# Trace of a batched matrix product: A resident per batch, two adjacent rows per partition, B streamed by row tile

## The chip, the cores and the metric

The kernel runs on one core of one Trainium2 chip. The metric is device time in microseconds (us), the median of several executions. A profile shows a span that is about 1.7 us shorter than the timed execution, because it runs from the first to the last instruction.

Some words: TensorE is the engine for matrix products and, here, for transposes; it writes into a memory called PSUM, from which VectorE reads. GpSimd issues the transfers. A row tile is 128 rows of a matrix, one per partition of the on-chip memory. A descriptor is the order to move one contiguous run of bytes. A landing is the record that a part of a transfer has arrived. The granted clock is TensorE's, as a share of full speed.

## The reference

```python
def setup_inputs():
    B, N = 8, 2176
    # a, b: random normal, float32, shape (8, 2176, 2176)

def reference(a, b):
    prod = np.matmul(a, b)
    traces = np.diagonal(prod, axis1=1, axis2=2).sum(axis=-1)
    return traces.astype(np.float32)
```

The trace of A·B is the sum over all i and j of A[i, j]·B[j, i]. No matrix product is needed. One of the two matrices must be transposed, multiplied with the other element by element, and summed. All of A and B must be read: 303.04 MB in fp32.

## The kernel before

N is 17 tiles of 128 (NT = 17). A whole row tile is one transfer, which casts fp32 to bf16 on the way. B comes in groups of four row tiles, with buffers for two groups. TensorE transposes 128x128 blocks of B into PSUM, and VectorE multiplies four of them with 512 columns of A and sums.

```python
    KGW = 4                                  # row tiles of B in a group
    a_pool = ctx.enter_context(tc.tile_pool(name="a_pool", bufs=2 * NT))
    b_pool = ctx.enter_context(tc.tile_pool(name="b_pool", bufs=2 * KGW))
    psum_pool = ctx.enter_context(tc.tile_pool(name="psum", bufs=7, space=bass.MemoryType.PSUM))
    # ... (cut)
    for bi in range(BATCH):
        a_tiles = []
        for j_blk in range(NT):
            a_tile = a_pool.tile([P, N], dt, tag="a")
            nc.gpsimd.dma_start(out=a_tile, in_=a[bi, j_blk * P:(j_blk + 1) * P, :])
            a_tiles.append(a_tile)
        # ... (cut)
        for kg in range(N_KG):
            # ... (cut) kc_lo, kc_hi: the row tiles of this group
            for kc in range(kc_lo, kc_hi):
                b_tile = b_pool.tile([P, N], dt, tag="b")
                nc.gpsimd.dma_start(out=b_tile, in_=b[bi, kc * P:(kc + 1) * P, :])
                b_chunks.append(b_tile)
            for j_blk in range(NT):
                psum_tile = psum_pool.tile([P, F], dt, tag="bT")
                for i, b_tile in enumerate(b_chunks):
                    nc.tensor.transpose(psum_tile[:, i * P:(i + 1) * P],
                                        b_tile[:, j_blk * P:(j_blk + 1) * P], identity)
                # ... (cut) scratch
                nc.vector.tensor_tensor_reduce(   # sum of a * bT over the group's columns
                    out=scratch[:, :fw], in0=a_tiles[j_blk][:, kc_lo * P:kc_hi * P],
                    in1=psum_tile[:, :fw], # ... (cut)
                    accum_out=acc[:, j_blk * N_KG + kg: j_blk * N_KG + kg + 1])
```

VectorE cannot start on a group before all four of its row tiles are there.

## Time and profile before

| | before |
|---|---|
| time, median | 737.29 us (737.23 to 737.42) |
| span of the profile | 735.6 us |
| busy: TensorE, VectorE, GpSimd | 37%, 50%, 20% of the span |
| bytes read | 303.04 MB |
| chain of waits: share of transfers | 80% |

The page's GB/s figure counts the bytes written, which are half of those read. In the chain of waits a share of 80% for transfers says that the last instruction is reached mostly over waits for data. The lines themselves are in the prediction below.

### The profile page before, as it was taken

How to read it: one execution, taken by the hardware profiler on the slowest of the kernel's cores; microseconds unless marked ns; L12 is line 12 of the kernel's file. 1: busy time of each engine (PE TensorE's matmuls, PEld its weight loads, DVE VectorE, ACT ScalarE, POOL GpSimd, SP SyncE). 2: the span in 40 equal slices, each digit the busy share in tenths (PEclk: the TensorE clock that was granted, in tenths of full speed). 3: DMA queues.
4: the chain of work that ended last, by engine and by line, in shares of the span. 5: the costliest groups of instructions: out<-in, count | busy, mean ns of one | idle time of the engine just before them, and what ended most of it. 6: DMA issues, size and time to landing. Idle time of an engine off the chain costs nothing.

```text
span 735.6 us, 7232 instructions
## 1 busy us (share of the span) xinstructions
PE 271.7 (37%) x2314; PEld 217.7 (30%) x2314; DVE 364.8 (50%) x1370; POOL 144.4 (20%) x278
## 2 busy tenths in 40 slices
PE   0016441174412744035450453505453054520665
PEld 0005430163301533024340343403342034410454
DVE  0007673087610967019570285704766056750698
POOL 4221221112121221212222122221222222221110
PEclk9999775557655556556655556555556556665575
DMA  8999999999999999999999999999999999999891
GB/s 175 213 214 215 213 215 213 214 214 214 214 213 214 214 214 214 213 214 213 214 214 213 214 213 214 214 213 215 213 214 214 213 214 214 214 214 213 161 209 29
DMA packets 39208, 152.00 MB, mean 207 GB/s; under 512 B 4354, under 2 KB 4354, under 8 KB 39170
## 3 DMA queue, kind: packets, MB, share of 16 engines
q0 software_dynamic: 39168, 151.54, 102.2%
q8 instruction: 18, 0.29, 0.1%
q14 instruction: 20, 0.16, 0.1%
q1 hardware_dynamic: 2, 0.00, 0.0%
HBM read 303.04 MB, written 0.00 MB: 412 GB/s over the span
## 4 chain that ended last, share of the span: by engine, by line
DMA 80%; issue 16%; POOL 1%; DVE 1%; PE 0%; POOLq 0%; DVEq 0%
DMA b_tile<-in_b_dram 51%; DMA a_tile<-in_a_dram 29%; POOL b_tile L66 1%; DVE scratch L78 1%; DVE acc L78 1%; POOL a_tile L52 0%; PE psum_tile L72 0%; POOLq L66 0%; POOL identity masks.py:199 0%; DVE batch_accs L89 0%; PE batch_psum L94 0%; DVEq L78 0%; POOL identity masks.py:197 0%; DVE result_tile L95 0%; POOLq masks.py:199 0%
## 5 line engine op out<-in xcount | busy, mean ns | idle before, releaser
L78 DVE CUSTOM_DVE_ANT_0 scratch<-a_tile,psum_tile 128x512 bf16<-128x512 bf16 (+1 forms) x680 | 362.3, 602 | 367.4 <-PE psum_tile L72 367.2
L72 PE MATMUL psum_tile<-identity,b_tile 128*128 128x128 bf16 x2312 | 271.5, 286 | 460.3 <-DMA b_tile<-in_b_dram 434.1
L72 PEld LDWEIGHTS <-b_tile 128*128 128x128 bf16 x2312 | 217.6, 132 | 513.8 <-DMA b_tile<-in_b_dram 465.6
L66 POOL DMA_DIRECT2D b_tile<-in_b_dram x136 | 71.8, 532 | 332.6 <-PE psum_tile L72 180.2
L52 POOL DMA_DIRECT2D a_tile<-in_a_dram x136 | 72.2, 533 | 238.0 <-DMA b_tile<-in_b_dram 112.4
L78 DVE DVE_READ_ACCUMULATOR2_ANT acc<- 128x1 f32 x680 | 55.9, 82 | 0.0
L89 DVE TENSOR_REDUCE batch_accs<-acc 128x1 f32<-128x85 f32 x8 | 1.9, 241 | 0.3
L94 PE MATMUL batch_psum<-batch_accs,ones 128*1 128x8 f32 x2 | 0.2, 173 | 1.5 <-DVE batch_accs L89 1.5
L94 PEld LDWEIGHTS batch_psum<-batch_accs,ones 128*1 128x1 f32 x2 | 0.1, 80 | 1.8 <-DVE batch_accs L89 1.8
L37 DVE MEMSET ones<- 128x1 f32 x1 | 0.1, 59 | 0.8 <-PEq L115 0.8
masks.py:199 POOL TENSOR_SCALAR_AFFINE_SELECT identity<-identity 128x128 bf16<-128x128 bf16 x1 | 0.3, 305 | 0.1
L95 DVE COPY result_tile<-batch_psum 1x8 f32<-1x8 f32 x1 | 0.2, 155 | 0.3 <-PE batch_psum L94 0.3
masks.py:197 POOL MEMSET identity<- 128x128 bf16 x1 | 0.2, 204 | 0.3 <-POOLq L115 0.3
L115 POOL MEMSET const-float32-0.0<- 128x1 f32 x1 | 0.1, 98 | 0.2 <-issue 0.2
L115 POOL MEMSET const-bfloat16-1.0<- 128x1 bf16 x1 | 0.1, 101 | 0.0
L115 POOL MEMSET const-uint8-127<- 128x1 uint8 x1 | 0.1, 101 | 0.0
L115 POOL MEMSET const-float32-1.0<- 128x1 f32 x1 | 0.1, 98 | 0.0
## 6 DMA issues: line engine op xcount, KB each, us to landing
a_tile<-in_a_dram POOLq DMA_DIRECT2D x136, 544.0 KB, 20.6
b_tile<-in_b_dram POOLq DMA_DIRECT2D x136, 544.0 KB, 20.3
out_dram<-result_tile SPq DMA_DIRECT2D x1, 0.0 KB
```

What stands on the lines that cost most here:

```text
L37: nc.vector.memset(ones, 1.0)
L52: nc.gpsimd.dma_start(out=a_tile, in_=a[bi, j_blk * P:(j_blk + 1) * P, :])
L66: nc.gpsimd.dma_start(out=b_tile, in_=b[bi, kc * P:(kc + 1) * P, :])
L72: nc.tensor.transpose(psum_tile[:, i * P:(i + 1) * P], b_tile[:, j_blk * P:(j_blk + 1) * P], identity,)
L78: nc.vector.tensor_tensor_reduce(out=scratch[:, :fw], in0=a_tiles[j_blk][:, kc_lo * P:kc_hi * P], in1=psum_tile[:, :fw], scale=1.0, scalar ...
L89: nc.vector.reduce_sum(out=batch_accs[:, bi:bi + 1], in_=acc, axis=mybir.AxisListType.X)
L94: nc.tensor.matmul(batch_psum, ones, batch_accs, start=True, stop=True)
L95: nc.vector.tensor_copy(out=result_tile[:1, :BATCH], in_=batch_psum)
L115: nc = _bacc.Bacc("TRN2", target_bir_lowering=False, num_devices=1)
```

## The change

The change wants the transfers to be cheaper and the end shorter. Each partition takes two adjacent matrix rows, so one descriptor reads 17,408 B in place of 8,704 B. A row of the matrix is then not a partition number any more, so columns of B are read with step two to match A, and columns of A with step two to match B. A is one tile per batch, loaded a batch ahead. B is consumed by row tile, with wider VectorE ops (768 and 640 columns). In the last batch B comes in single rows, and the last two tiles in four pieces each.

```diff
+    CHUNKS = [(0, 6), (6, 12), (12, NT)]
+    LAST_CHUNKS = [(0, 6), (6, 12), (12, 16), (16, NT)]
-    a_pool = ctx.enter_context(tc.tile_pool(name="a_pool", bufs=2 * NT))
-    b_pool = ctx.enter_context(tc.tile_pool(name="b_pool", bufs=2 * KGW))
+    a_pool = ctx.enter_context(tc.tile_pool(name="a_pool", bufs=2))
+    b_pool = ctx.enter_context(tc.tile_pool(name="b_pool", bufs=5))
 ... (cut)
+    groups = row_groups(N, P, ROWS)          # ROWS = 2: (first row, rows per partition)
+    slot_cols = [(start + r, m) for start, m in groups for r in range(m)]
+    def load(dst, src, start, m):
+        rows = src[start:start + P * m, :].rearrange("(p r) k -> p r k", r=m)
+        nc.gpsimd.dma_start(out=dst, in_=rows)
 ... (cut: load_a; the A of batch 0 is loaded ahead of everything)
+        for gi, (start, m) in enumerate(b_groups):
+            b_tile = b_pool.tile([P, ROWS, N], dt, tag="b")
+            pieces = last and gi >= len(b_groups) - 2
+            chunks = LAST_CHUNKS if pieces else CHUNKS
+            if pieces:
+                for lo, hi in chunks:
+                    nc.gpsimd.dma_start(
+                        out=b_tile[:, 0, lo * P:hi * P],
+                        in_=b[bi, start:start + P, lo * P:hi * P],
+                    )
+            else:
+                load(b_tile[:, 0:m, :], b[bi], start, m)
+            if not last:
+                load_a(a_next, bi + 1, gi)
+            for lo, hi in chunks:
+                for s in range(m):
 ... (cut: w = hi - lo)
+                    psum_tile = psum_pool.tile([P, 6, P], dt, tag="bT")
+                    for u in range(lo, hi):
+                        c0, step = slot_cols[u]
+                        nc.tensor.transpose(
+                            psum_tile[:, u - lo, :],
+                            b_tile[:, s, c0:c0 + step * (P - 1) + 1:step],
+                            identity,
+                        )
 ... (cut: scratch)
+                    nc.vector.tensor_tensor_reduce(
+                        out=scratch[:, :w, :],
+                        in0=a_all[:, lo:hi, start + s:start + s + m * (P - 1) + 1:m],
+                        in1=psum_tile[:, :w, :],
 ... (cut)
```

More of the change, by code (lines that the diff above doesn't have):

```diff
@@ L5, with row_groups @@
 import concourse.tile as tile
-from concourse import bass_utils, mybir
-from concourse import bass_isa
+from concourse import mybir
 from concourse.masks import make_identity
 from concourse._compat import with_exitstack
+def row_groups(n, p, rows):
+    groups, at = [], 0
+    while at < n:
+        m = min(rows, (n - at) // p)
+        groups.append((at, m))
+        at += m * p
+    return groups
 @with_exitstack
@@ L22 @@
     BATCH, N, N2 = a.shape
-    assert N == N2
-    assert N % P == 0
+    assert N == N2 and N % P == 0
     NT = N // P
-    KGW = 4
-    F = KGW * P
-    N_KG = (NT + KGW - 1) // KGW
+    ROWS = 2
+    CHUNKS = [(0, 6), (6, 12), (12, NT)]
+    LAST_CHUNKS = [(0, 6), (6, 12), (12, 16), (16, NT)]
     dt = mybir.dt.bfloat16
+    f32 = mybir.dt.float32
     const = ctx.enter_context(tc.tile_pool(name="const", bufs=1))
+    a_pool = ctx.enter_context(tc.tile_pool(name="a_pool", bufs=2))
+    b_pool = ctx.enter_context(tc.tile_pool(name="b_pool", bufs=5))
@@ new lines @@
+    psum_pool = ctx.enter_context(tc.tile_pool(name="psum", bufs=7, space=bass.MemoryType.PSUM))
+    psum_small = ctx.enter_context(tc.tile_pool(name="psum_small", bufs=1, space=bass.MemoryType.PSUM))
+    scratch_pool = ctx.enter_context(tc.tile_pool(name="scratch", bufs=2))
+    acc_pool = ctx.enter_context(tc.tile_pool(name="acc", bufs=2))
+    groups = row_groups(N, P, ROWS)
[3 more added lines that the diff above has]
+        nc.gpsimd.dma_start(out=dst, in_=rows)
@@ L34, with load_a @@
+    def load_a(a_all, bi, gi):
+        start, m = groups[gi]
+        slot = start // P
+        load(a_all[:, slot:slot + m, :], a[bi], start, m)
+    a_next = a_pool.tile([P, NT, N], dt, tag="a")
+    for gi in range(len(groups)):
+        load_a(a_next, 0, gi)
     identity = const.tile([P, P], dt, tag="identity")
     make_identity(nc, identity)
-    ones = const.tile([P, 1], mybir.dt.float32, tag="ones")
+    ones = const.tile([P, 1], f32, tag="ones")
     nc.vector.memset(ones, 1.0)
-    batch_accs = const.tile([P, BATCH], mybir.dt.float32, tag="batch_accs")
@@ L39 @@
-    result_tile = const.tile([P, BATCH], mybir.dt.float32, tag="result")
-    a_pool = ctx.enter_context(tc.tile_pool(name="a_pool", bufs=2 * NT))
-    b_pool = ctx.enter_context(tc.tile_pool(name="b_pool", bufs=2 * KGW))
-    psum_pool = ctx.enter_context(tc.tile_pool(name="psum", bufs=7, space=bass.MemoryType.PSUM))
-    psum_small = ctx.enter_context(tc.tile_pool(name="psum_small", bufs=1, space=bass.MemoryType.PSUM))
-    scratch_pool = ctx.enter_context(tc.tile_pool(name="scratch", bufs=4))
@@ L46 @@
-    acc_pool = ctx.enter_context(tc.tile_pool(name="acc", bufs=2))
-    for bi in range(BATCH):
-        a_tiles = []
-        for j_blk in range(NT):
-            a_tile = a_pool.tile([P, N], dt, tag="a")
-            nc.gpsimd.dma_start(out=a_tile, in_=a[bi, j_blk * P:(j_blk + 1) * P, :])
-            a_tiles.append(a_tile)
-        acc = acc_pool.tile([P, NT * N_KG], mybir.dt.float32, tag="acc")
-        for kg in range(N_KG):
-            kc_lo = kg * KGW
-            kc_hi = min(kc_lo + KGW, NT)
-            gw = kc_hi - kc_lo
-            fw = gw * P
-            b_chunks = []
-            for kc in range(kc_lo, kc_hi):
-                b_tile = b_pool.tile([P, N], dt, tag="b")
-                nc.gpsimd.dma_start(out=b_tile, in_=b[bi, kc * P:(kc + 1) * P, :])
-                b_chunks.append(b_tile)
-            for j_blk in range(NT):
-                psum_tile = psum_pool.tile([P, F], dt, tag="bT")
-                for i, b_tile in enumerate(b_chunks):
-                    nc.tensor.transpose(
-                        psum_tile[:, i * P:(i + 1) * P],
-                        b_tile[:, j_blk * P:(j_blk + 1) * P],
-                        identity,
-                    )
-                scratch = scratch_pool.tile([P, F], dt, tag="scr")
-                nc.vector.tensor_tensor_reduce(
-                    out=scratch[:, :fw],
-                    in0=a_tiles[j_blk][:, kc_lo * P:kc_hi * P],
-                    in1=psum_tile[:, :fw],
-                    scale=1.0,
-                    scalar=0.0,
-                    op0=mybir.AluOpType.mult,
-                    op1=mybir.AluOpType.add,
-                    accum_out=acc[:, j_blk * N_KG + kg: j_blk * N_KG + kg + 1],
-                )
@@ new lines @@
+    batch_accs = const.tile([P, BATCH], f32, tag="batch_accs")
+    result_tile = const.tile([P, BATCH], f32, tag="result")
+    for bi in range(BATCH):
+        a_all = a_next
+        last = bi == BATCH - 1
+        b_groups = row_groups(N, P, 1 if last else ROWS)
+        acc = acc_pool.tile([P, NT * len(LAST_CHUNKS)], f32, tag="acc")
+        col = 0
+        if not last:
+            a_next = a_pool.tile([P, NT, N], dt, tag="a")
+        for gi, (start, m) in enumerate(b_groups):
[7 more added lines that the diff above has]
+                        in_=b[bi, start:start + P, lo * P:hi * P],
+                    )
+            else:
+                load(b_tile[:, 0:m, :], b[bi], start, m)
+            if not last:
+                load_a(a_next, bi + 1, gi)
+            for lo, hi in chunks:
+                for s in range(m):
+                    w = hi - lo
+                    psum_tile = psum_pool.tile([P, 6, P], dt, tag="bT")
[6 more added lines that the diff above has]
+                        )
+                    scratch = scratch_pool.tile([P, 6, P], dt, tag="scr")
+                    nc.vector.tensor_tensor_reduce(
+                        out=scratch[:, :w, :],
+                        in0=a_all[:, lo:hi, start + s:start + s + m * (P - 1) + 1:m],
+                        in1=psum_tile[:, :w, :],
+                        scale=1.0,
+                        scalar=0.0,
+                        op0=mybir.AluOpType.mult,
+                        op1=mybir.AluOpType.add,
+                        accum_out=acc[:, col:col + 1],
+                    )
+                    col += 1
@@ L89 @@
         nc.vector.reduce_sum(
-            out=batch_accs[:, bi:bi + 1], in_=acc, axis=mybir.AxisListType.X
+            out=batch_accs[:, bi:bi + 1], in_=acc[:, :col], axis=mybir.AxisListType.X
         )
-    batch_psum = psum_small.tile([1, BATCH], mybir.dt.float32, tag="bp")
+    batch_psum = psum_small.tile([1, BATCH], f32, tag="bp")
     nc.tensor.matmul(batch_psum, ones, batch_accs, start=True, stop=True)
```

## The prediction

> **What bounds the kernel now.** I read the page from the top. Busy shares first: TensorE 37%, VectorE 50%, GpSimd 20%, so no compute engine is near the span. Then the slices, the DMA queue line and the chain of waits:
>
> ```profile
> DMA  8999999999999999999999999999999999999891
> GB/s 175 213 214 215 213 215 213 214 214 214 214 213 214 214 214 214 213 214 213 214 214 213 214 213 214 214 213 215 213 214 214 213 214 214 214 214 213 161 209 29
> ...
> q0 software_dynamic: 39168, 151.54, 102.2%
> ...
> DMA 80%; issue 16%; POOL 1%; DVE 1%; PE 0%; POOLq 0%; DVEq 0%
> ```
>
> Each GB/s figure covers 18.4 us and counts bytes written (bf16); the reads are fp32, twice that. The rate is a flat 213 to 215 in all slices but four: the first (175), one at 161, one at 209 and the last (29). So the DMA engines are the bound, and what can be won is (a) those slices and (b) the flat rate itself. The byte count cannot change: the reference needs all of A and B, 303.04 MB.
>
> Two more views size these. The stretches of the end, then the last instructions in the timeline (columns of a stretch: PE, PEld, DVE and POOL busy with counts, clock, DMA share, GB/s):
>
> ```profile
> 660.00:680.00 20.00, 0.93 (x7) 0.66 (x7) 0.00 (x0) 3.69 (x7) 0.50 1.06 213
> 680.00:700.00 20.00, 12.27 (x93) 9.50 (x94) 13.08 (x43) 2.11 (x4) 0.50 0.84 166
> 700.00:710.00 10.00, 5.43 (x60) 4.44 (x59) 9.32 (x31) 2.12 (x4) 0.84 1.05 211
> ...
> 720.00:722.00 2.00, 2.00 (x21) 2.00 (x20) 2.00 (x9) 0.00 (x0) 0.50 0.03 7
> 724.00:736.00 12.00, 5.30 (x36) 2.69 (x33) 9.32 (x54) 0.00 (x0) 0.64 0.00 1
> ```
>
> ```profile
> 693.69 2.11 POOL L66 DMA_DIRECT2D b_tile<-in_b_dram  x4 [16.52 <-PE psum_tile L72]
> ...
> 732.96 0.24 DVE L89 TENSOR_REDUCE batch_accs<-acc 128x1 f32<-128x85 f32 x1
> 733.49 0.15 DVE L95 COPY result_tile<-batch_psum 1x8 f32<-1x8 f32 x1 [0.29 <-PE batch_psum L94]
> 733.67 0.31 SPq L97 DMA_DIRECT2D out_dram<-result_tile  x1
> ```
>
> In the last batch there is no A to fetch. GpSimd has no B buffer free (8 buffers, in groups of 4) until TensorE has transposed a whole group, and waits 16.52 us for it. Of that, the DMA engines lose 20 x (1 - 166/213) = **4.4 us**. Data stops near 720.9 us (last data packet record), yet the span ends at 735.6: **14.7 us** of tail in which VectorE works off the last group of four row tiles and then the odd 17th.
>
> **The flat rate.** From the packet records of the trace: all 34,816 data packets write 4,352 B (one matrix row); on one engine they start 323.5 ns apart, and each transfer ends in a 4-byte semaphore packet that costs 21.5 ns more. A transfer is 8 data packets per engine: 8 x 323.5 + 21.5 = 2,609.5 ns. The timeline agrees: single B tiles land at 409.59, 412.19, 414.81 and 417.43 us, 2.61 us apart. Check: 272 x 2.6095 = 709.8, plus some 1.6 us for instruction fetches (44 packets of the other queues, their times over 16 engines), plus 2.64 us until the first data packet, plus the 4.4 us gap and under 1 us around the 715 us mark = 719 us, against 720.9 seen. The sum closes within 2 us.
>
> **What the Trainium skill says, and the trace.**
> 1. "DMA: Bandwidth & Descriptors", section Where 436 GB/s comes from: 32 B per cycle at 850 MHz and engine. A row of 8,704 B is 272 beats, 320.0 ns. The same page, section Why small descriptors are slow: some 3 cycles fixed per packet, 3.5 ns. Sum 323.5 ns: exactly the measured pitch.
> 2. "VectorE: DVE Perf Modes", The perf-mode tier table: an elementwise op of two tensors with one in PSUM runs at 1x, 0.96 GHz. The trace agrees: the 128x512 op follows itself every 0.608 us and the 128x128 op every 0.207, a slope of 401/384 = 1.04 ns per column and 0.07 us fixed. At 1x there is no packed mode for step two to lose.
> 3. "SBUF — State Buffer", Specifications: 16-byte lines, at least two hits per line for full rate. Step two in bf16 gives four hits. No run shows a strided operand yet.
> 4. "TensorE: Matmul & The Clock Gate", Weight-path perf modes: the fast weight load takes packed or strided columns. Again the trace has only packed ones.
>
> **The change part by part.**
>
> *Larger descriptors.* A pair of rows is 17,408 B in one run, 544 beats + 3 cycles = 643.5 ns (estimate from point 1). A pair transfer: 8 x 643.5 + 21.5 = 5,169.5 ns, against 2 x 2,609.5 = 5,219: **-49.5 ns**. There are 8 x 8 pairs of A and 7 x 8 of B (the last batch's B stays in single rows): 120 x 49.5 = **-5.9 us**, wholly on the path.
>
> *The new transfers summed.* 120 x 5.1695 = 620.3; 8 singles of A, 7 of B and 15 of the last batch, 30 x 2.6095 = 78.3; the last two tiles in four pieces each, (334 ns of data x 8 + 4 x 21.5) x 2 = 5.5. Together 704.2, plus 1.5 of instruction fetches = 705.7 us.
>
> *Start.* The A loads are written ahead of the identity. The first issue now starts at 1.27 us, the first data is at 2.64; I allow 0.3 us gained: first data at 2.3.
>
> *The gap of the last batch goes.* B is now consumed row tile by row tile, and a buffer comes free after 17 transposes, some 17 x 104 ns = 1.8 us (61 matmuls took 6.32 us in the burst at 718.63). Five buffers then leave three or more in flight. **-4.4 us**.
>
> *The tail shrinks.* VectorE per row tile: two ops of 768 columns and one of 640, 0.874 + 0.874 + 0.74 = 2.49 us by the slope above, against 2.61 us of DMA in the last batch (5.2 us in the others, where A comes too). So VectorE is level with the data at the end. The last tile's pieces land within the last 1.7 us; working forward, the first piece is done about 0.1 us after the last landing, the second at 1.0, the third (512) at 1.6, the last (128) at 1.8. Then reduce, matmul, copy and output: before took 2.64 us from the reduce's start to the end, and about 0.1 us goes before it. Tail about **4.6 us** instead of 14.7.
>
> *Instructions.* VectorE ops drop from 680 to 8 x 51 + 2 = 410, transposes stay 2,312. Both were hidden; no gain on the path by itself.
>
> *Sum.* 2.3 + 705.7 + about 0.6 (the slowest engine ends later than the median one, as before) + 4.6 = 713.2 us of span. Timed runs were 737.29 - 735.6 = 1.7 above the profiled span: **about 715 us**. I take 715.5, leaning to small new gaps.
>
> **The rivals.**
>
> *A. Descriptors give nothing.* If the generator cuts the pair back into two packets of 8,704 B, only the saved semaphore packets count: 120 x 21.5 ns = 2.6 us, so 718.5. If something at the memory side sets the 323.5 ns, nothing: 721. For it: no run here shows a larger packet. Against: the pitch is beats plus three cycles to the half nanosecond.
>
> *B. A wait at each batch change.* A whole A buffer comes free only when VectorE has finished the batch before last, and GpSimd issues in order, so the first A load of each new batch blocks everything behind it. When the last B tile of a batch lands, only one single A (2.6 us) and one B pair (5.2 us) are queued: 7.8 us. TensorE and VectorE need about 3.4 us for that tile, then 1.4 us from issue to first data, 4.8 to 5.5 us with wake-ups. It fits by some 2 us; if a strided A operand slowed VectorE to half, it would not, and six changes at about 1 us each would give 721.
>
> *C. TensorE or VectorE becomes the bound in the last batch.* 17 transposes have 2.61 us, 153 ns each, against 104 now at the low clock. If strided weights took 200 ns, the batch would take 17 x 17 x 0.2 = 58 us instead of 44: about 729. VectorE has only 5% to spare there; 10% slower ops cost 2 us. For it: nothing measured on step two. Against: points 2 to 4.
>
> *D. The tail was hidden anyway.* It cannot be: nothing transfers after 721 us, and every microsecond there is the span's.
>
> **Range and chances.** Even with no gain from descriptors (A at worst) the gap and the tail give 737.3 - 4.4 - 10.1 - 0.3 = 722.5, just at the line of 2%; the descriptors add 2.6 to 5.9. B and C could take back 6 to 14 us, at about one chance in eight together. So 715.5 us, 711 to 722; faster by over 2% 0.89, within 2% 0.10, slower 0.01.
>
> **What would show it.** Data packets: about half as many, each of 8,704 B, some 643 ns apart; two-row transfers landing 5.17 us apart; the flat rate 215 instead of 213 to 214 GB/s. No slice below 210 between the first and the last. GpSimd's waits on TensorE gone in the last batch. VectorE's 768-column op following itself in 0.87 us whether strided or not. The data's end near 708.6 us and the span's end 4 to 5 us later. The prediction is wrong if packets stay at 4,352 B, if the rate dips at batch changes with GpSimd waiting on VectorE, or if TensorE is continuously busy over the last 45 us.

## The result, and the profile after

The changed kernel takes **720.23 us** (median of 4 runs, 720.03 to 720.28) against 737.26 us of the kernel before in the same rounds. The ratio is 0.9768, with a 95% interval of 0.9754 to 0.9782. The result is correct. The predicted direction and range (711 to 722) held; the time is 4.7 us above the predicted 715.5.

The page of the changed kernel, slices and DMA lines, and the first line of the chain of waits:

```profile
DMA  8999999999999999999999999999999999999995
GB/s 177 215 214 216 216 217 215 214 217 216 216 216 215 215 216 216 215 216 215 216 215 214 216 216 216 215 214 217 216 215 215 214 218 216 214 216 214 213 214 100
DMA packets 22784, 151.92 MB, mean 212 GB/s; under 512 B 2786, under 2 KB 3554, under 8 KB 7394
...
q0 software_dynamic: 22752, 151.53, 101.4%
q8 instruction: 18, 0.29, 0.1%
q14 instruction: 12, 0.10, 0.0%
...
DMA 93%; issue 3%; PE 2%; DVE 1%; POOL 0%; POOLq 0%; ACTq 0%
```

Three things are to be seen. The flat rate rose from 213 to 215 up to 213 to 218, mostly 214 to 217. The packets went from 39,208 to 22,784. And the last full slice is at 214 and the very last at 100, where before had 161, 209 and 29. The two "instruction" queues fetch the engines' programs; they will matter below.

The stretches of the end of the changed kernel (length, PE, PEld, DVE and POOL busy with counts, granted clock, DMA share, GB/s):

```profile
690.00:700.00 10.00, 6.36 (x67) 5.49 (x66) 9.82 (x23) 2.52 (x5) 0.67 1.04 211
700.00:705.00 5.00, 3.34 (x37) 2.91 (x36) 4.92 (x13) 2.38 (x6) 0.70 1.09 207
705.00:707.00 2.00, 0.75 (x14) 0.58 (x11) 2.00 (x5) 0.40 (x1) 1.00 1.16 196
707.00:709.00 2.00, 1.12 (x17) 0.95 (x17) 2.00 (x7) 0.53 (x1) 1.00 0.87 144
709.00:711.00 2.00, 1.47 (x17) 0.97 (x17) 2.00 (x5) 0.00 (x0) 1.00 0.42 63
711.00:713.00 2.00, 1.02 (x12) 0.68 (x12) 2.00 (x9) 0.00 (x0) 1.00 0.07 11
```

The transfers do not stop together. From 707 us the rate falls in steps, 144, 63, 11: fewer and fewer of the 16 DMA engines are still at work. The last data packet ends at 712.86 us. The timeline of the very end:

```profile
712.37 0.34 PEld L103 LDWEIGHTS <-b_tile 128*128 128x128 bf16 x6 [0.60 <-DMA b_tile<-in_b_dram]
...
715.30 0.28 DVE L109 CUSTOM_DVE_ANT_0 scratch<-a_next,psum_tile 128x128 bf16<-128x128 bf16 x1
...
715.63 0.21 DVE L121 TENSOR_REDUCE batch_accs<-acc 128x1 f32<-128x53 f32 x1
...
716.31 0.31 SPq L129 DMA_DIRECT2D out_dram<-result_tile  x1
```

The first pieces' transposes of the last tile had to wait for a landing until 712.37. VectorE's last product ends at 715.6 and the span at 718.2, so the tail after the last data is 5.4 us, in place of 14.7.

**Where the 17.3 us of span went** (735.58 to 718.24). The data ends 8.0 us earlier (720.88 to 712.86), and the tail is 9.3 us shorter (14.7 to 5.4). The prediction had 12.3 and 10.1. So the open question is the data's end: 708.6 us predicted, 712.86 measured.

**A view of the lag.** Each transfer lands in 16 parts, one per DMA engine, and the landing records of the trace give each. The difference between the first and the last part is how far the slowest engine lies behind the fastest:

```text
changed kernel: us of landing, spread over the 16 engines (us)
 168.1  1.86 |  246.0  2.19 |  324.1  2.72 |  402.2  3.24 |  485.4  3.76
 563.5  4.29 |  600.3  4.85 |  673.3  5.35 |  712.3  5.67
kernel before:
 154.0  1.66 |  259.3  2.78 |  375.1  3.80 |  481.0  5.36 |  586.4  6.42
 691.7  7.35 |  699.6  1.18 (just after the gap of the last batch)
```

The spread grows in steps of about 0.53 us, each just after an 8 KB fetch of the q14 queue (at 308, 377, 448, 523, 593 and 666 us among others). The records give no engine number, but the offsets can be followed from one transfer to the next, and they fit one engine that falls further behind: it starts 0.64 us after the fastest, and stands at 1.17, 1.7, 2.23 and so on up to 5.38 us after the fetches at 90, 154, 230, 308, 377, 448, 523, 593 and 666 us. The 1.86 us at the start belong to another engine, which this one overtakes at 230 us. Two of the 12 fetches (177 and 586 us) don't move it. In the kernel before, the spread reached 7.35 us, and the gap of the last batch let the slow engine catch up. The prediction had read that gap as a pure loss and had taken 0.6 us for the lag.

### The profile page after: what moved, and what is told of

The parts are those of the page before. It is cut to its first block, busy times and chain, and to the rows that moved or that the text cites. A ratio compares the mean times of both kernels' runs of the same rounds, so it can differ in the third digit from the quotient of the medians.

```text
span 718.2 us, 6176 instructions
## 1 busy us (share of the span) xinstructions
PE 248.2 (35%) x2314; PEld 228.3 (32%) x2314; DVE 347.1 (48%) x830; POOL 84.6 (12%) x164
## 3 DMA queue, kind: packets, MB, share of 16 engines
q0 software_dynamic: 22752, 151.53, 101.4%
## 4 chain that ended last, share of the span: by engine, by line
DMA 93%; issue 3%; PE 2%; DVE 1%; POOL 0%; POOLq 0%; ACTq 0%
DMA b_tile<-in_b_dram 86%; DMA a_next<-in_a_dram 7%; PE psum_tile L103 2%; DVE scratch L109 1%; POOL a_next L54 0%; DVE acc L109 0%; DVE batch_accs L121 0%; POOLq L54 0%; PE batch_psum L126 0%; DVE result_tile L127 0%; ACTq L158 0%
## 5 line engine op out<-in xcount | busy, mean ns | idle before, releaser
L109 DVE CUSTOM_DVE_ANT_0 scratch<-a_next,psum_tile 128x768 bf16<-128x768 bf16 (+1 forms) x410 | 344.7, 903 | 367.8 <-PE psum_tile L103 367.0
L103 PE MATMUL psum_tile<-identity,b_tile 128*128 128x128 bf16 x2312 | 248.0, 302 | 465.5 <-DMA b_tile<-in_b_dram 459.4
L103 PEld LDWEIGHTS <-b_tile 128*128 128x128 bf16 x2312 | 228.2, 143 | 485.1 <-DMA b_tile<-in_b_dram 485.1
L54 POOL DMA_DIRECT2D a_next<-in_a_dram x72 | 38.7, 542 | 329.3 <-DVE batch_accs L121 157.1
L54 POOL DMA_DIRECT2D b_tile<-in_b_dram x78 | 41.7, 535 | 286.1 <-DMA b_tile<-in_b_dram 151.0
L109 DVE DVE_READ_ACCUMULATOR2_ANT acc<- 128x1 f32 x410 | 34.0, 83 | 0.0
L87 POOL DMA_DIRECT2D b_tile<-in_b_dram x8 | 4.2, 537 | 7.6 <-DMA b_tile<-in_b_dram 4.1
L121 DVE TENSOR_REDUCE batch_accs<-acc 128x1 f32<-128x51 f32 (+1 forms) x8 | 1.7, 206 | 0.3
```

The source lines that it names most:

```text
L54: nc.gpsimd.dma_start(out=dst, in_=rows)
L87: nc.gpsimd.dma_start(out=b_tile[:, 0, lo * P:hi * P], in_=b[bi, start:start + P, lo * P:hi * P],)
L103: nc.tensor.transpose(psum_tile[:, u - lo, :], b_tile[:, s, c0:c0 + step * (P - 1) + 1:step], identity,)
L109: nc.vector.tensor_tensor_reduce(out=scratch[:, :w, :], in0=a_all[:, lo:hi, start + s:start + s + m * (P - 1) + 1:m], in1=psum_tile[:, :w, :],
L121: nc.vector.reduce_sum(out=batch_accs[:, bi:bi + 1], in_=acc[:, :col], axis=mybir.AxisListType.X)
```

## The experiments

Theory, formed on the traces: (1) packets cost three cycles each, as predicted; (2) instruction fetches that fall on one DMA engine make it late, and the last tile lands when that engine is done; (3) the gap of the last batch cost nothing, as VectorE set the end there and the slow engine needed the time anyway. Rivals: the end is late because of the small last pieces; one engine is slow by itself; the gap was worth 4.4 us; the order of the work gave everything and the descriptors nothing. Each experiment ran 5 rounds against the kernel before, whose medians were 737.30 to 737.47. The intervals of e4, e6 and e8 overlap with that of the changed kernel, but their single runs don't: none of theirs lies in its 720.03 to 720.28.

| run | what | us | ratio to before (95%) |
|---|---|---|---|
| changed kernel | | 720.23 | 0.9768 (0.9754 to 0.9782) |
| e1_apart | descriptors of one row | 723.69 | 0.9813 (0.9800 to 0.9827) |
| e2_twice | TensorE instructions nearly doubled | 720.21 | 0.9766 (0.9753 to 0.9779) |
| e3_fewer | fewer TensorE and VectorE instructions, wrong result | 717.66 | 0.9731 (0.9718 to 0.9745) |
| e4_whole_last | last tiles whole | 720.73 | 0.9774 (0.9761 to 0.9787) |
| e5_dve_more | 714 more VectorE instructions | 723.57 | 0.9814 (0.9801 to 0.9828) |
| e6_two_banks | fewer, longer VectorE ops | 718.98 | 0.9752 (0.9738 to 0.9765) |
| e7_before_b12 | before with 12 buffers for B | 737.12 | 0.9999 (0.9986 to 1.0011) |
| e8_quads | A in fours | 718.53 | 0.9745 (0.9732 to 0.9759) |
| e9_quads_two | e6 and e8 together | 717.38 | 0.9731 (0.9718 to 0.9744) |

### e1_apart: the descriptors alone undone

```diff
-        rows = src[start:start + P * m, :].rearrange("(p r) k -> p r k", r=m)
+        rows = src[start:start + P * m, :].rearrange("(r p) k -> p r k", r=m)
-    slot_cols = [(start + r, m) for start, m in groups for r in range(m)]
+    slot_cols = [(start + r * P, 1) for start, m in groups for r in range(m)]
-                        in0=a_all[:, lo:hi, start + s:start + s + m * (P - 1) + 1:m],
+                        in0=a_all[:, lo:hi, start + s * P:start + s * P + P],
```

> The changed kernel with the two rows of a partition 128 rows apart, so that each transfer has the same bytes but 8,704 B descriptors and columns of step one. Theory (packet overhead of three cycles each, as in the prediction): 120 pair transfers each pay 8 more packets of 3.5 ns per engine, 28 ns, so data ends 3.4 us later and the time is 723.6 us; data packets 4,352 B every 323.5 ns. Rival (the descriptor size gives nothing; all of the gain is the order of the work): 720.2 us within 0.5. If step two slowed VectorE or TensorE, the 768-column op would now be shorter than its 0.874 us pitch.

Measured: 723.69 us, 3.46 us above the changed kernel. Its data packets are one row again, 323.5 ns apart on one engine; in the changed kernel they are two rows and 643.5 ns apart, as estimated. The page's packet line and data queue of e1:

```profile
DMA packets 38144, 151.92 MB, mean 210 GB/s; under 512 B 2786, under 2 KB 3554, under 8 KB 38114
...
q0 software_dynamic: 38112, 151.53, 103.9%
```

The bytes are the same 151.53 MB, the packets 38,112 in place of 22,752. Of the 17.0 us between the kernel before and the changed one, the larger packets give 3.5, and all the rest of the change 13.6 (737.26 - 720.23 - 3.46); this run doesn't divide the rest. Step two also shows its price here: none. The groups of the 768-column VectorE op, first of the changed kernel (step two in seven batches), then of this run (step one):

```profile
L109 DVE CUSTOM_DVE_ANT_0 scratch<-a_next,psum_tile 128x768 bf16<-128x768 bf16 x272 | 244.3, 951 | 367.8 <-PE psum_tile L103 367.0
```

```profile
L109 DVE CUSTOM_DVE_ANT_0 scratch<-a_next,psum_tile 128x768 bf16<-128x768 bf16 x272 | 244.3, 950 | 371.7 <-PE psum_tile L103 371.0
```

951 against 950 ns. The 17 weight loads of a row tile take 1.73 us at the low clock in both.

### e2_twice: many more TensorE instructions

```diff
-                        nc.tensor.transpose(
+                        for _ in range(2 if not last and gi < 8 else 1):
+                            nc.tensor.transpose(
```

> The changed kernel with each transpose of the row pairs of the first seven batches issued twice, to the same place: 1,904 more pairs of weight load and matmul, all hidden behind the transfers (TensorE about 3.6 us per row tile against 5.2). Theory (instruction fetches for TensorE land on single DMA engines and make one engine lag, seen as the spread between engines growing by some 0.53 us per batch): 15 more 16 KB fetches beside 18, so the lag of the slowest engine at the end grows by about 80%, data ends some 3 us later, 723 us. Rival (one engine is slower by itself, or the lag comes from the small last pieces): 720.2 us within 0.5, spread between engines as before.

Measured: 720.21 us, no change. The instruction queues, from its page:

```profile
q8 instruction: 33, 0.54, 0.3%
q14 instruction: 12, 0.10, 0.0%
```

The theory in its first form missed. TensorE's fetches are the q8 queue: 18 became 33, and the time stayed. The landing records say why. A 16 KB fetch delays an engine by about 1.0 us, but the delays show on several engines in turn. Before the last tile seven of the 16 were within 1.1 us of the fastest and nine were 4.5 to 5.3 us behind it, but none was later than the slowest had been (5.67 us in the changed kernel). The engine that ended the data in the changed kernel moved with q14, and q14 still had 12. So the theory was narrowed to q14.

### e3_fewer: fewer instructions of both (wrong result)

```diff
-            for lo, hi in chunks:
+            for lo, hi in (chunks if last else chunks[:1]):
                 for s in range(m):
```

> Wrong result on purpose: in the first seven batches only the first 6 of 17 column blocks are transposed and multiplied; all transfers stay. Theory (fetch lag): 1,309 transposes fewer, about 10 of 18 fetches of 16 KB gone, so data ends some 2 us earlier, about 718 us. Rival (the lag is of the engine itself): the same 720.2 within 0.5. Rival of hidden compute on the path in the middle: more than 3 us gained.

Measured: 717.66 us, 2.6 us faster, with a wrong result. Its instruction queues:

```profile
q8 instruction: 8, 0.13, 0.1%
q14 instruction: 6, 0.05, 0.0%
```

q14 went from 12 to 6, the spread before the last tile from 5.67 to 3.0 us, and the data's end from 712.86 to 709.87 us. The time followed nearly all of it. That the expected 718 us came out is luck: it counted ten fewer fetches of 16 KB, which are q8's, and e2 shows that these do not move the time here. One engine that is slow by itself is ruled out: up to 580 us, with three fetches before that, the spread stays between 1.59 and 1.93 us, but for five single landings of 2.3 to 2.4 at q8 fetches. By itself this run also cut the work of TensorE and VectorE and the q8 fetches (18 to 8), so it needed e5 beside it, and e2 for q8.

### e4_whole_last: without the small pieces

```diff
-            pieces = last and gi >= len(b_groups) - 2
+            pieces = False
```

> The changed kernel with the last two row tiles of B loaded whole instead of in four pieces. Theory: less packet and semaphore cost (0.3 us), but the last tile lands whole at the end of the data, then 0.9 us of transposes and 2.5 us of VectorE follow: 1.0 to 1.5 us slower, 721.5 us. Rival (the small pieces themselves cost the 3 us by which data ended late): 717.5 us.

Measured: 720.73 us, 0.5 us slower; the single runs (720.65 to 720.90) lie apart from the changed kernel's, the intervals do not. The data ended at 712.53 us, so the pieces are not why it ends late; the rival (717.5 us) is out. They are worth 0.5 us at most, not the 1.0 to 1.5 that was expected.

### e5_dve_more: more VectorE instructions alone

```diff
                     col += 1
+                    if not last:
+                        nc.vector.memset(junk, 0.0)      # junk: 128x1
+                        nc.vector.memset(junk, 0.0)
```

> The changed kernel with two tiny fills of a 128x1 tile after each VectorE op of the first seven batches: 714 more VectorE instructions, some 43 us of work, hidden there (VectorE is half idle). Theory (every 8 KB fetch of the second instruction queue, which follows the number of VectorE instructions, delays the same DMA engine by about 0.53 us, and that engine ends the data): 714 x 64 B is 5.6 more fetches, the slowest engine ends its share 3 us later, 723 us. Rival (fetches have nothing to do with the lag; VectorE in the first seven batches is hidden): 720.2 us within 0.5.

Measured: 723.57 us, 3.3 us slower (the profiled run took 722.99). Its page, and a stretch of the last batch:

```profile
PE 255.8 (35%) x2314; PEld 235.0 (33%) x2314; DVE 387.1 (54%) x1544; POOL 84.4 (12%) x164
...
q8 instruction: 18, 0.29, 0.1%
q14 instruction: 17, 0.14, 0.0%
```

```profile
650.00:690.00 40.00, 20.85 (x192) 18.66 (x191) 28.25 (x67) 4.75 (x9) 0.63 1.03 205
```

This is the cleanest test: beside VectorE's own count only q14 moved, 12 to 17, and the time with it. VectorE is 54% busy, far from a bound. The spread reached 7.70 us at 676 us: a start of 0.33 us and 14 steps of 0.53 are 7.75. Then the other engines had to wait: by 694 us the spread had fallen to 5.3 us, and the rate is down to 205 GB/s in this stretch, while the slowest engine's landings stayed some 2.6 us apart. The reason is argued, not tested: in the last batch a buffer comes free only when the slowest engine's share has landed and been used, and GpSimd waits for one before each of its issues there.

### e6_two_banks: fewer, longer VectorE ops

```diff
-    CHUNKS = [(0, 6), (6, 12), (12, NT)]
+    CHUNKS = [(0, 9), (9, NT)]
-    psum_pool = ... bufs=7 ...       psum_tile = psum_pool.tile([P, 6, P], dt, tag="bT")
+    psum_pool = ... bufs=3 ...       psum_tile = psum_pool.tile([P, 16, P], dt, tag="bT")
 ... (cut: scratch from 6 to 9 blocks)
```

> The changed kernel with VectorE ops of 9 and 8 column blocks over two banks of PSUM in place of 6, 6 and 5: 272 + 8 fewer VectorE instruction pairs. Theory (fetch lag plus VectorE's pace in the last batch): about 2 fetches fewer, 1.1 us less lag, and 0.07 us per row tile off VectorE's chain, so 1 to 2 us faster, 718.7 us. Rival (three PSUM tiles in place of seven let TensorE fall behind): 720.5 or more.

Measured: 718.98 us, 1.25 us faster, correct. (The 272 + 8 of the expectation are instructions, not pairs: the page has 562 for VectorE in place of 830, 268 fewer.) q14 fell to 9 fetches, the spread before the last tile to 4.4 us, the data's end to 711.4 us. Four runs now give the time over the q14 fetches: 6, 9, 12, 17 fetches go with 717.66, 718.98, 720.23, 723.57 us. That is 0.4 to 0.7 us for each, about the 0.53 us of a step in the spread. e6 also shortens VectorE's chain in the last batch, and the run does not separate the two.

### e7_before_b12: the gap taken out of the kernel before

```diff
-    b_pool = ctx.enter_context(tc.tile_pool(name="b_pool", bufs=2 * KGW))
+    b_pool = ctx.enter_context(tc.tile_pool(name="b_pool", bufs=3 * KGW))
```

> The kernel before with 12 buffers for B in place of 8, nothing else. This takes away the 16.5 us wait of GpSimd in the last batch and with it the gap of the transfers. The prediction's reckoning (the gap is worth 4.4 us of the end): 733 us. Rival (VectorE, which runs without a pause from the landing of the first group of four to the end, 45 us, sets the end; the gap is hidden behind it): 737.3 us within 0.5.

Measured: 737.12 us, ratio 0.9999: nothing. The stretches of its end:

```profile
680.00:700.00 20.00, 12.21 (x92) 9.45 (x93) 13.02 (x43) 3.69 (x7) 0.50 1.06 214
700.00:710.00 10.00, 5.60 (x62) 4.68 (x60) 9.49 (x31) 0.53 (x1) 0.84 1.06 214
710.00:720.00 10.00, 6.88 (x67) 6.33 (x65) 10.00 (x35) 0.00 (x0) 0.67 0.48 96
720.00:730.00 10.00, 7.30 (x63) 5.92 (x61) 10.00 (x41) 0.00 (x0) 0.67 0.01 3
```

The gap is gone: 214 GB/s where the kernel before had 166. VectorE's busy time is the answer (third figure with a count): in the stretches from 700 to 730 us it works 9.5 to 10 of every 10 us, as it did (9.3 to 10) in the kernel before, where this line of the timeline starts a chain that runs to the end with under 0.8 us of pauses:

```profile
686.90 0.69 DVE L78 CUSTOM_DVE_ANT_0 scratch<-a_tile,psum_tile 128x512 bf16<-128x512 bf16 x1 [32.63 <-PE psum_tile L72]
```

From there VectorE has 4 groups of 17 ops at 0.608 us and 17 at 0.207 us, 44.9 us, and that sets the end whatever the transfers do. The last data did not come earlier either (720.7 us): without the gap the slow engine was 7.9 us behind the fastest. Both parts of the theory are seen in one run: the end is VectorE's, and the gap had not delayed the slowest engine's data.

### e8_quads and e9_quads_two: what the theory is good for

```diff
-    groups = row_groups(N, P, ROWS)
+    groups = row_groups(N, P, 4)
-            if not last:
-                load_a(a_next, bi + 1, gi)
+            if not last and gi % 2 == 1:
+                load_a(a_next, bi + 1, gi // 2)
+            if not last and gi == len(b_groups) - 1:
+                load_a(a_next, bi + 1, len(groups) - 1)
```

> The changed kernel with A in groups of four adjacent rows, 34,816 B descriptors and columns of step four; B as it is. Theory (three cycles per packet, one semaphore packet per transfer): 32 transfers of four rows each save 8 x 3.5 x 2 + 21.5 = 49.5 ns against two pairs on B's side of the same bytes, so data 1.6 us earlier, 718.6 us. Rival (descriptors over some length are cut up again): only the 0.7 us of semaphores, 719.5. Rival (step four costs TensorE or VectorE more): the pitch of VectorE's ops or the 104 ns of the transposes grows.

Measured: 718.53 us, 1.7 us faster, correct, with packets of four rows 1,283.5 ns apart on one engine (1,088 beats and three cycles). The size agrees with the theory. (The formula in the expectation has a factor 2 too many; 8 x 3.5 + 21.5 gives its 49.5 ns.) Step four costs nothing either: 951 ns for the 768-column VectorE op, 1.74 us for 17 weight loads. It isn't quite clean: the rate now dips to 209 to 212 GB/s about once per batch, and the spread at the end was only 3.8 us, so a part of the gain may be lag that such a pause let an engine make up.

e9 is e8 and e6 together.

> Both changes that gained, together: A in groups of four adjacent rows and VectorE ops over two banks of PSUM. Theory: the gains add, since one shortens every engine's data and the other takes away fetches from the slowest engine: 720.2 - 1.7 - 1.2 = 717.3 us, the fastest version here. Rival (VectorE's chain in the last batch, which starts with the first B tile landed and takes 42 us, becomes the bound and takes one of the two back): 718.2 us.

Measured: **717.38 us**, correct, the fastest version here: 0.9731 of the kernel before, 2.85 us under the changed kernel. The gains add.

## Why the prediction was right, point by point

- **Transfers bound the kernel: right, with one exception that it had in its own hands.** In the last batch of the kernel before VectorE set the end, not the transfers (e7). The prediction named VectorE's work as the tail, but did not say that this work runs from 686.9 us on.
- **Larger descriptors, -5.9 us: right as far as shown.** The packets are 643.5 ns apart, as estimated, and two-row transfers land 5.17 us apart. e1 shows the packet part, 3.46 us against 3.4; the semaphore part (2.6 us) was not tried alone. Rival A is out.
- **"The gap of the last batch goes, -4.4 us": the step that failed.** e7 took the gap out and gained 0.2 us, and its data ended at 720.7 us as before (720.9). The gap was in the mean over the engines. The slowest engine, 7.35 us behind, did not wait in it: its landings at 694.33, 696.98 and 699.56 us are 2.6 us apart, as always.
- **"About 0.6 (the slowest engine ends later than the median one, as before)": the term that was mis-sized.** Before, the gap had just brought the engines together, so the lag was small at the one place where the prediction read it. With the gap gone, the slowest engine is 5.67 us behind the fastest at the end, and some 3.3 us behind the middle ones. This is where the data's end at 712.86 in place of 708.6 us comes from: start 2.6 us plus 704.2 us of transfers is 706.8, and the fastest engine has its share of the last tile's third piece at 707.36. The slowest has it 5.6 us later: 0.64 us from the start, nine steps of 0.53 and a last one of 0.3. The prediction spread its fetches over 16 engines (1.5 us, from 44 packets of which the page counts 40 in the span); ten of them fell on one.
- **Start, 0.3 us gained: wrong, but small.** The first issue stood at 1.24 us and the first data at 2.60, against 1.27 and 2.64.
- **Tail, 4.6 us: nearly right,** 5.4 measured. VectorE was without a pause from 703 us on, so the last pieces queued. No run undoes the consumption by row tile alone, so the 9.3 us of the tail are read from the two profiles.
- **"GpSimd's waits on TensorE gone in the last batch": did not come true.** It waits before each of its issues there from 661 to 702 us, 9.8 us at most, yet the slices there stay at 213 and 214 GB/s.
- **Rival B, a wait at each batch change: right to dismiss.** The waits are there, but the slices show no cost. From the waits of the changed kernel (who waited for what, us in total, times, longest):

```profile
POOL a_next L54 <- DVE batch_accs L121: 157.1, 6, 26.6
...
POOL b_tile L54 <- PE psum_tile L103: 54.5, 14, 9.8
```

  Six waits for VectorE, 157 us in all, and no slice of the middle is below 214 GB/s: enough was queued each time.
- **Rival C, TensorE or VectorE slower by step two: right to dismiss** (e1). VectorE is close to a bound in the last batch all the same: from 672 to 703 us its pauses are 0.12 us at most.

The 715.5 us came out 4.7 us low because the loss of the last batch was counted as something to be won, while it was the place where a late engine caught up. The errors add up rather than cancel: 4.3 us at the data's end and 0.8 in the tail, less the 0.5 that was added to 715. The Trainium skill, "Runtime: NRT & Kernel Launch", section Instruction fetch mechanics, says that each sequencer drives its own DMA queue to refill its instruction memory, at a cost that is "mostly hidden". For the engines this trace agrees: of VectorE's 367.8 us of idle time before its 768-column products, 367.0 are waits for TensorE's transposes. For the transfers it is not hidden in a kernel in which all 16 DMA engines are at work all the time: six fetches of 8 KB fewer on q14 go with 2.6 us less (e3), five more with 3.3 us more (e5).

Left open: why ten of q14's 12 fetches delay one engine while q8's delays go round (the records give no engine numbers), where the 1.86 us of spread in the first transfer come from, and how e6's gain divides between fewer fetches and a shorter chain.

## What to carry to other kernels

A transfer is done when the slowest of its 16 engines is done, so in a kernel bound by transfers look at the spread of the landings, not only at the mean rate; a gap in the mean rate may be the time in which the slowest engine catches up. Before counting such a gap as a gain, ask which wait ends last at the end of the kernel: here VectorE ran almost without pause from 686.9 us on. And fewer, longer instructions on an engine that is half idle can still save time, because its program comes over the same DMA engines as the data.

## What the Trainium skill lacked or had wrong

- "Runtime: NRT & Kernel Launch", Instruction fetch mechanics, calls the cost of a refill mostly hidden. Here an 8 KB refill puts the engine that it falls on about 0.53 us behind, and a 16 KB one about 1.0 us; 5 more 8 KB refills cost 3.3 us (e5), 15 more 16 KB ones nothing (e2).
- The same section gives blocks of 16 KiB. That fits the queue that follows TensorE (q8, 16 KB packets); the packets of q14 are 8 KB.
- "DMA: Bandwidth & Descriptors", Why small descriptors are slow, gives three cycles per packet with a 256 B example. It holds unchanged up to 34,816 B: 323.5, 643.5 and 1,283.5 ns for 272, 544 and 1,088 beats. So the overhead is still 1% at 8.7 KB, and worth 3.5 us here.
- The same page, Anatomy of one DMA, calls the bubble of the semaphore write about one cycle and "essentially free", and has no figure for the packet itself. Here it takes 21.5 ns per engine and transfer; 120 transfers saved are 2.6 us (estimate).
- The same page, Latency and other measured facts, names a best guess for engines that are usually slower than others. Here one engine is late too, and its lag follows the instruction fetches (3.0, 4.4 and 5.67 us of spread with 6, 9 and 12 of them). The records give no engine number, so no run shows whether it is one of those that the page names.
- "SBUF — State Buffer" and "TensorE: Matmul & The Clock Gate" let step two in bf16 pass without loss; no figure stood there. Measured: 951 against 950 ns for the VectorE op, 1.73 us for 17 weight loads either way; with step four (e8) 951 ns and 1.74 us.
